# A fixed order for the first stage of a two-layer hybrid encoder, gates in tiles, the softmax ahead

## The chip, the cores and the metric

One core of one Trainium2 chip runs the whole network in one launch. The metric is the device time of that launch in microseconds (us), the median of several runs. TensorE (PE) multiplies matrices; VectorE (DVE), ScalarE (ACT) and GpSimd (POOL) do the elementwise work; SyncE (SP) issues most transfers.

## The reference, cut to what matters

The input is 512 tokens by 1024 features in float32. Layer 0 has sliding-window attention with sinks beside an HGRN2 recurrence, layer 1 has chunked attention; each layer ends with a gated feed-forward network with a short convolution. The change touches layer 0 up to the end of its attention.

```python
y = rms_norm(h, nw[0])                      # per token, over 1024 features, times a weight
proj = y @ w_in                             # split into qa, ka, va, qb, fb, ib, gb
# HGRN2, per head of 128 keys, in blocks of 32 tokens:
f = lb + (1 - lb) * sigmoid(f_logit); k = 1 - f
q_dec = q * exp(cumsum(log f)); k_dec = k * exp(-cumsum(log f))
s = where(causal, q_dec @ k_dec.T, 0); o = s @ ib + q_dec @ state    # state decays per block
# sliding-window attention, per head and 128 queries, after rotary embedding:
m = max(max(s), sink); p = exp(s - m); p = p / (sum(p) + exp(sink - m)); o = p @ va
```

## The kernel before, in words

Activations lie with features on the partitions (`xs`, eight chunks of 128 features by 512 tokens), weights come in units of 128 x 1024 float32. A product keeps close to float32 by a split: `prep` (L197) loads a unit, ScalarE rounds it to a high part (L206), VectorE takes the rest as the low part (L207), and `mm3` (L235) multiplies three times, high by high (L238), then the two cross terms (L239, L240). So 128 tokens against a panel of 512 columns take 24 matmuls of 512 columns over the 1024 features.

The order on each engine is set by a planner that walks the instructions by priority at compile time and keeps a model of when each is ready; the list of background steps (`later`, `fill`, `need`) sets which projection is written between which steps of a head.

`start` (L364) is the first stage. It runs 17 warm-up matmuls, loads four tiles of 128 tokens (L386) and the norm weight spread over all partitions (L303), and for each tile takes the sum of squares (L309), the root (L324 to L328), the product with norm weight and root (L343 for the first tile, on POOL at L345 and ScalarE at L348 for the others), eight transposes (L354) and the split (L357, L358). `value_panel` (L502) then makes the recurrence's values, tile by tile, and copies them to `ib` (L512).

`even` (L516) runs, for each of four heads, the projections `forget` and `query` in `hgrn_in` (L569), then `hgrn` (L609). In `forget` VectorE scans the decay `F` (L583), takes one reciprocal of 128 x 512 (L584), multiplies it with `kk` (L585), POOL makes a second product (L587), and VectorE fills a small table `tab` (L589 to L592). In `hgrn` the products of keys and values come from L643, VectorE turns them into running states `S` (L648, L650), and PE uses these at L656, between matmuls of the block's own scores (L654).

Then comes the rotary embedding (`rope`, L671: L679 on VectorE, L680 on POOL, L681 adds) and the attention. Each step `score` (L706) writes 128 queries' scores (L714, L715), adds the mask and takes the maximum on VectorE (L721), combines it with the sink (L722), exponentiates on ScalarE (L723), and divides (L724, L725); some steps later PE transposes the result (L734).

Of the kernel before, what the change touches and what calls it, by code (L numbers as in the profile page):

```python
# [27 lines left out]
P = 128  # L28
T = 512
# [11 lines left out]
HB = 32  # L41
HALF = (slice(0, 64), slice(64, 128))
TOK = [slice(t * P, (t + 1) * P) for t in range(NT)]
FH = [slice(0, 512), slice(512, 1024)]
# [101 lines left out]
class Net:  # L146
# [50 lines left out]
    def prep(self, i):  # L197
        if i in self.prepped or i >= len(UNITS):
            return
        nc, n = self.nc, UNIT_W[i]  # L200
        raw = self.wp.tile([P, UW], F32, tag="raw", bufs=3, name=f"wr{i}")
        hi = self.wp.tile([P, UW], F32R, tag="hi", name=f"wh{i}")
        lo = self.wp.tile([P, UW], F32R, tag="lo", name=f"wl{i}")
        o = int(UNIT_OFF[i]) * P
        nc.sync.dma_start(raw[:, :n], self.w[o:o + n * P].rearrange("(p n) -> p n", p=P))
# [76 lines left out]
    def rsqrt(self, nv, n=1):  # L282

        v = self.nc.vector
        y, t = self.small(n, "rs"), self.small(n, "rt")
        v.tensor_scalar(y.bitcast(I32), nv.bitcast(I32), -0.5, RSQRT_SEED, op0=ALU.mult, op1=ALU.add)
        for _ in range(3):
            if n == 1:

                v.tensor_scalar(t, y, y, nv, op0=ALU.mult, op1=ALU.mult)  # L290
                v.tensor_scalar(y, t, 1.5, y, op0=ALU.add, op1=ALU.mult)
            else:
                v.tensor_mul(t, y, nv)
                v.tensor_mul(t, t, y)
                v.scalar_tensor_tensor(y, t, 1.5, y, op0=ALU.add, op1=ALU.mult)
# [40 lines left out]
    def pre_norm(self, t, src, w, x, first=False):  # L336
# [4 lines left out]
        if first:  # L341
            r = self.root(s)
            nc.vector.scalar_tensor_tensor(hw, src, r, w, op0=ALU.mult, op1=ALU.mult)  # L343
        else:
            nc.gpsimd.tensor_mul(hw, src, w)  # L345
            r = self.root(s)
            for f in FH:
                nc.scalar.mul(hw[:, f], hw[:, f], r)  # L348

        def turn():  # L350
            for a in range(2):
                ps = self.bank("t", 2)
                for k in range(4):
                    nc.tensor.transpose(ps[:, TOK[k]], hw[:, (4 * a + k) * P:(4 * a + k + 1) * P], self.ident)  # L354
                at = lambda z: z[:, 4 * a:4 * a + 4, TOK[t]]
                p3 = ps.rearrange("p (k n) -> p k n", n=P)
                nc.scalar.copy(at(x[0]), p3)  # L357
                nc.vector.tensor_sub(at(x[1]), p3, at(x[0]).bitcast(F32))  # L358
        return turn
# [4 lines left out]
    def start(self):  # L364
        nc = self.nc
        self.ident = self.cp.tile([P, P], F32, name="ident")
        zeros = self.hp.tile([P, D], F32, tag="h3", name="zeros").bitcast(BF16)[:, :T]
        self.pt = self.cp.tile([P, PT_W], F32, name="pt")
        self.pt, self.eps = self.pt[:, :PC_N], self.pt[:, PC_N:PC_N + 1]
        nc.vector.memset(zeros, 0.0)  # L370
        nc.vector.memset(self.eps, EPS)
        make_identity(nc, self.ident)

        warm = self.small(1, "warm")
        nc.vector.memset(warm, 0.0)
        nc.scalar.activation(warm, warm, AF.Sqrt)
        ps = self.bank("s", 2)

        def warm_up(n):
            for _ in range(n):  # L380
                nc.tensor.matmul(ps, zeros[:, 0:P], zeros, start=True, stop=True)

        warm_up(17)
        x = self.new_x()
        src = [self.yp.tile([P, D], F32, tag="y", name=f"x{t}") for t in range(NT)]
        load = lambda t: nc.sync.dma_start(src[t], self.x[TOK[t], :])  # L386
        load(0)
        w = self.norm_row(0, 0)
        load(1)
        for i in range(NT):  # L390
            self.prep(i)
        load(2)
# [3 lines left out]
        for t in range(NT):  # L396
            self.turns[t] = self.pre_norm(t, src[t], w, x, t == 0)
            if t == 0:
                self.turn(0)
                warm_up(3)  # L400
        return self.chunks(x)
# [114 lines left out]
    def even(self, xs):  # L516
        nc, tc = self.nc, self.tc
        with tc.tile_pool(name="ev", bufs=2) as ep:
# [14 lines left out]
            lg = self.pt[:, PC_LB:PC_LB + 8]  # L533
            mx, e0, e1 = fix(4), fix(4), fix(4)
            nc.vector.tensor_max(mx, lg[:, 0:4], lg[:, 4:8])
            nc.vector.tensor_sub(e0, lg[:, 0:4], mx)
            nc.vector.tensor_sub(e1, lg[:, 4:8], mx)
            nc.scalar.activation(e0, e0, AF.Exp)
            nc.scalar.activation(e1, e1, AF.Exp)
            nc.vector.tensor_add(mx, e0, e1)  # L540
            nc.vector.reciprocal(mx, mx)
            c0, c1 = fix(4), fix(4)
            nc.vector.tensor_mul(c0, e0, mx)
            nc.vector.tensor_scalar(c1, c0, -0.5, 0.5, op0=ALU.mult, op1=ALU.add)
            nc.vector.tensor_scalar(c0, c0, 0.5, 0.5, op0=ALU.mult, op1=ALU.add)
            sink, nsink, hgn = self.pt[:, PC_SINK:PC_SINK + 8], fix(8), fix(4)
# [476 lines left out]
```

## Time and profile before

| | |
|---|---|
| median of 3 runs | 1220.49 us (1220.44 to 1220.56) |
| the profiled execution's own time | 1220.75 us |
| its span, first to last instruction | 1219.0 us |
| mean granted TensorE clock | 0.997 of 2.4 GHz |
| busy: PE, VectorE, ScalarE, POOL | 98%, 53%, 44%, 11% |

How to read it: busy time is the union of an engine's instructions in the span. A matmul's end is modelled, so PE can be called busy while the next matmul is already overdue; the distance from one matmul's start to the next one's is the surer measure. A row of the timeline gives start, duration, engine, line, operation, tiles written and read, a count, and in brackets the idle time before it and what ended that.

### The profile page before, as it was taken

Reading aid. Unit: us, or ns where it says so; the run is one execution under the profiler, and the core shown is the slowest. Engines: PE = TensorE matmul, PEld = TensorE weight load, DVE = VectorE, ACT = ScalarE, POOL = GpSimd, SP = SyncE. Lnnn points to the kernel's source line nnn. Section 1 sums busy time; section 2 is a strip of 40 time slices with the busy share of each in tenths; the row PEclk is TensorE's granted clock in tenths of the full one; section 3 lists DMA queues with packets and bytes.
Section 4 is the critical chain, followed back from the end, with each engine's and each line's share of the span. In section 5 each row is a group of like instructions: output and inputs, shape, how many; then the busy total and the mean of one; then the engine's idle time right before and its main releaser. Section 6 shows DMA issues by size and latency. Waiting matters only on the chain.

```text
span 1219.0 us, 15387 instructions
## 1 busy us (share of the span) xinstructions
PE 1198.4 (98%) x5804; PEld 982.6 (81%) x5804; DVE 649.9 (53%) x1317; ACT 536.9 (44%) x979; POOL 131.5 (11%) x127
## 2 busy tenths in 40 slices
PE   8999999999999999999999999999999999999997
PEld 5878777898888888888887777778888888888886
DVE  6687785755542244453457766756544522444434
ACT  6334564653332233333556656556533322333331
POOL 4233210320000000001420000003200000000011
PEclk9999999999999999999999999999999999999999
DMA  7413311234222332222243223212332223332211
GB/s 251 137 54 113 113 62 52 81 128 137 87 95 81 112 110 87 104 89 84 80 132 105 75 60 121 96 51 87 115 121 103 80 95 104 104 104 87 95 61 70
DMA packets 35595, 119.53 MB, mean 98 GB/s; under 512 B 4160, under 2 KB 4288, under 8 KB 35520
## 3 DMA queue, kind: packets, MB, share of 16 engines
q1 hardware_dynamic: 34944, 117.49, 29.3%
q8 instruction: 46, 0.75, 0.2%
q10 hardware_dynamic: 576, 1.05, 0.2%
q14 instruction: 29, 0.24, 0.1%
HBM read 115.12 MB, written 2.10 MB: 96 GB/s over the span
## 4 chain that ended last, share of the span: by engine, by line
PE 85%; DVE 6%; ACT 3%; issue 3%; POOL 2%; DMA 1%; SPq 0%; DVEq 0%; ACTq 0%; POOLq 0%
PE ps_mm L238 17%; PE ps_mm L239 17%; PE ps_mm L240 17%; PE ps_s L238 4%; PE ps_s L239 4%; PE ps_s L240 4%; PE ps_po L238 3%; PE ps_po L240 3%; PE ps_po L239 3%; PE ps_mm L956 2%; PE ps_po L902 2%; PE ps_t L891 1%; DVE wl L207 1%; POOL hw L345 1%; DVE hg L584 1%
## 5 line engine op out<-in xcount | busy, mean ns | idle before, releaser
L207 DVE TENSOR_TENSOR wl<-wr,wh 128x1024 fp32r<-128x1024 f32 (+1 forms) x191 | 235.9, 1237 | 319.3 <-ACT wh L206 314.0
L206 ACT CAST wh<-wr 128x1024 fp32r<-128x1024 f32 x198 | 204.4, 1035 | 371.2 <-PE ps_mm L239 116.0
L238 PE MATMUL ps_mm<-xh,wh 128*128 128x512 f32 x608 | 242.8, 399 | 0.0
L239 PE MATMUL ps_mm<-xl,wh 128*128 128x512 f32 x608 | 238.1, 392 | 0.0
L240 PE MATMUL ps_mm<-xh,wl 128*128 128x512 f32 x608 | 237.9, 391 | 0.0
L240 PEld LDWEIGHTS ps_mm<-xh,wl 128*128 128x128 f32 x608 | 114.2, 188 | 24.1 <-issue 0.4
L238 PEld LDWEIGHTS ps_mm<-xh,wh 128*128 128x128 f32 x608 | 114.5, 188 | 21.3 <-issue 0.9
L239 PEld LDWEIGHTS ps_mm<-xl,wh 128*128 128x128 f32 x608 | 114.5, 188 | 20.0
L238 PE MATMUL ps_mm<-wh,ah 128*128 128x512 f32 x264 | 102.8, 389 | 0.0
L240 PE MATMUL ps_mm<-wh,al 128*128 128x512 f32 x264 | 102.7, 389 | 0.0
L239 PE MATMUL ps_mm<-wl,ah 128*128 128x512 f32 x264 | 102.7, 389 | 0.0
L437 POOL TENSOR_TENSOR y<-y,nw 128x512 f32<-128x512 f32 x16 | 22.2, 1394 | 675.6 <-ACT junk L309 675.6
L238 PE MATMUL ps_s<-xh,wh 128*128 128x512 f32 x208 | 80.9, 389 | 0.0
L239 PE MATMUL ps_s<-xl,wh 128*128 128x512 f32 x208 | 80.9, 389 | 0.0
L240 PE MATMUL ps_s<-xh,wl 128*128 128x512 f32 x208 | 80.9, 389 | 0.0
L932 ACT ACTIVATE g<-g 128x512 f32<-128x512 f32 x44 | 27.8, 632 | 84.0 <-DVE g L931 84.0
L240 PEld LDWEIGHTS ps_mm<-wh,al 128*128 128x128 f32 x264 | 49.5, 188 | 10.3
L239 PEld LDWEIGHTS ps_mm<-wl,ah 128*128 128x128 f32 x264 | 49.5, 188 | 10.3
L238 PEld LDWEIGHTS ps_mm<-wh,ah 128*128 128x128 f32 x264 | 49.6, 188 | 10.2
L933 DVE TENSOR_TENSOR a<-ps_mm,g 128x512 f32<-128x512 f32 x32 | 22.1, 692 | 55.7 <-PE ps_mm L240 55.4
L879 ACT ACTIVATE pr<-pr,m 128x128 f32<-128x128 f32 (+1 forms) x64 | 36.0, 563 | 33.7 <-DVE m L878 33.2
L240 PEld LDWEIGHTS ps_s<-xh,wl 128*128 128x128 f32 x208 | 39.0, 188 | 8.2
(245 smaller groups left out, 2065.6 us busy)
## 6 DMA issues: line engine op xcount, KB each, us to landing
wr<-in_w SPq DMA_DIRECT2D x190, 512.0 KB, 3.5
nw<-in_nw SPq DMA_DIRECT2D x8, 512.0 KB, 4.2
bt<-in_relb SPq DMA_DIRECT2D x16, 256.0 KB, 3.2
x<-in_x SPq DMA_DIRECT2D x4, 512.0 KB, 5.5
h<-in_x SPq DMA_DIRECT2D x4, 512.0 KB, 3.5
wr<-in_w SPq DMA_DIRECT2D x8, 256.0 KB, 2.5
rope<-rope SPq DMA_DIRECT2D x20, 64.0 KB, 2.0
out<-h SPq DMA_DIRECT2D x4, 256.0 KB, 2.0
```

What stands on the lines that cost most here:

```text
L206: nc.scalar.copy(hi[:, :n], raw[:, :n])
L207: (nc.gpsimd if i in POOL_LO else nc.vector).tensor_sub(lo[:, :n], raw[:, :n], hi[:, :n].bitcast(F32))
L238: mm(ps, a[0], b[0], start=start, stop=False, skip_group_check=skip)
L239: mm(ps, a[0], b[1], start=False, stop=False, skip_group_check=skip)
L240: mm(ps, a[1], b[0], start=False, stop=stop, skip_group_check=skip)
L345: nc.gpsimd.tensor_mul(hw, src, w)
L437: nc.gpsimd.tensor_mul(z, z, wy[:, FH[f]])
L879: nc.scalar.activation(p_, p_, AF.Exp, bias=m, accum_out=den)
L902: nc.tensor.matmul(po[rows, j * P:], v[j][:, o:o + 64], pT[g][:, po_[j]:po_[j] + T - j * P], start=j == 0, stop=j == 3, skip_group_check=True)
L932: nc.scalar.activation(g, g, AF.Gelu)
L933: nc.vector.tensor_mul(a, pv, g)
L956: nc.tensor.matmul(ps[:, hf], u[wi][:, k, :], xs[k][xi][:, hf], start=i == k == 0, stop=i == 2 and k == KD - 1, skip_group_check=True)
```

## The change

The first stage is written as one method, `opening`, in a block where PE, VectorE and ScalarE keep the written order. The first token tile is multiplied raw: transposed as loaded, weighted by the norm weight per partition while it leaves PSUM (`weighted`), and multiplied in plain float32 with the unsplit weight units (`plain`, eight matmuls of 512 columns); its root is applied to the result, and to the tile itself later, by a product with a row of roots that PE spreads with a matmul of ones. The second tile is scaled by its root, transposed, and weighted per partition in the same way. The third and fourth are scaled by VectorE alone. The warm-up falls from 17 and 3 matmuls to 7, 1 and 2. The transfers are issued in the order x0, norm row (8 x 128, from ScalarE's queue), units 0 and 1, x1, units 2 and 3, x2, spread norm weight, x3, parameters, and units 0 to 2 land in buffers that are free, so none of these waits. What follows the opening (units 4 to 6, the small gate constants) is issued behind its last instructions.

In `forget` the table comes before the reciprocal, and reciprocal and product run in four tiles of 128 columns. In `hgrn` the copy of the transposed keys and the states `S` get a priority of 300 ahead, in `score` the whole softmax. The sine product of the rotary embedding moves from POOL to VectorE.

```diff
-        def turn():
-            for a in range(2):
-                ps = self.bank("t", 2)
...
+        load(0)
+        nc.scalar.dma_start(rows, self.nw[0, 0].rearrange("(k n) -> k n", n=P))
+        self.fetch(0, raw[0])
+        self.fetch(1, raw[1])
+        load(1)
+        self.fetch(2, raw[2])
+        self.fetch(3, raw[3])
+        load(2)
+        w = self.norm_row(0, 0)
+        load(3)
...
+        def scaled(t):
+            hw[t] = self.wide("hw")
+            for f in FH:
+                nc.vector.scalar_tensor_tensor(hw[t][:, f], src[t][:, f], r[t], w[:, f], op0=ALU.mult, op1=ALU.mult)
...
+        def weighted(out, ps):
+
+            for a in range(2):
+                nc.vector.tensor_mul(p3(out[:, FH[a]]), p3(ps[a]),
+                                     wcol[:, 4 * a:4 * a + 4].unsqueeze(2).to_broadcast([P, 4, P]))
...
+        with self.tc.manual_schedule(engines={E.PE, E.DVE, E.Activation}):
...
+            warm_up(7)
...
+            pt = [self.turn_half(src[0], a) for a in range(2)]
+            warm_up(2)
+            weighted(x0, pt)
+            nc.scalar.copy(hi[0], raw[0])
+            part_lo(0)
+            nc.scalar.copy(hi[1], raw[1])
+            part_lo(1)
+            r[1] = self.root(self.square_sum(src[1]))
+            p0 = self.bank("mm", 3)
+
+            def plain(k):
+                nc.tensor.matmul(p0, x0[:, TOK8[k]], raw[k // 2][:, FH[k % 2]], start=k == 0, stop=k == KD - 1)
+
+            for k in range(5):
+                plain(k)
+            hw[1] = self.wide("hw")
+            pt = []
+            for a in range(2):
+                nc.vector.tensor_scalar_mul(hw[1][:, FH[a]], src[1][:, FH[a]], r[1])
+                pt.append(self.turn_half(hw[1], a))
+            for k in range(5, KD):
+                plain(k)
+            nc.scalar.copy(hi[2], raw[2])
+            x1 = self.wide("x1")
+            weighted(x1, pt)
...
+            r[2] = self.root(self.square_sum(src[2]))
+            scaled(2)
...
+            p1 = self.tok(ps1, xs, us, 1, True, True)
+            for _ in range(7):
+                next(p1)
+            self.to_features(2, hw[2], x)
+            self.run_all(p1)
+            r[0] = self.root(self.square_sum(src[0]))
+            r[3] = self.root(self.square_sum(src[3]))
+            scaled(3)
...
+            p2 = self.tok(ps2, xs, us, 2, True, True)
+            for _ in range(6):
+                next(p2)
+            self.to_features(3, hw[3], x)
+
+            pr = self.bank("po", 1)
+            nc.tensor.matmul(pr[:, 0:P], ones, diag, start=True, stop=True)
+            self.run_all(p2)
+            x3 = p3(x0)
+            nc.vector.tensor_mul(x3, x3, pr[:, 0:P].unsqueeze(1).to_broadcast([P, KD, P]))
+            for a in range(2):
+                nc.scalar.copy(at(x[0], 0, a), x3[:, 4 * a:4 * a + 4])
+                end = [nc.vector.tensor_sub(at(x[1], 0, a), x3[:, 4 * a:4 * a + 4], at(x[0], 0, a).bitcast(F32))]
+            end.append(nc.scalar.copy(ib[2], ps2))
+
+        self.opened = [i.ins for i in end]
+        with self.behind():
+            for i in range(4, 7):
+                self.prep(i)
+        ps3 = self.bank("mm", 3)
+        self.run_all(self.tok(ps3, xs, us, 3, True, True))
...
-                    nc.vector.reciprocal(kd, F)
-                    nc.vector.tensor_mul(kd, kd, kk)
...
+                    for t in range(NT):
+                        nc.vector.reciprocal(kd[:, TOK[t]], F[:, TOK[t]])
+                        nc.vector.tensor_mul(kd[:, TOK[t]], kd[:, TOK[t]], kk[:, TOK[t]])
+
+                    nc.gpsimd.tensor_mul(blk(f2), blk(kd), blk(F)[:, :, HB - 1:].to_broadcast([P, T // HB, HB]))
...
+                with self.tc.high_priority(AHEAD):
+                    for t in range(NT - 1):
+                        S.append(ep.tile([P, P], F32, tag="S", bufs=3, name="S"))
...
-                    nc.gpsimd.tensor_mul(sw, sw, cst[:, CC_SIN:CC_SIN + T])
+                    nc.vector.tensor_mul(sw, sw, cst[:, CC_SIN:CC_SIN + T])
...
+                with self.tc.high_priority(AHEAD):
+                    nc.vector.tensor_tensor_reduce(p_, ps[:, :n], am[:, 256 - n:], 1.0, NEG, ALU.add, ALU.max, m)
+                    nc.vector.tensor_scalar(nm, m, -1.0, nsink[:, hh:hh + 1], op0=ALU.mult, op1=ALU.min)
```

## Rows read from the trace of the kernel before

**Rows 1.** The page: busy time of the engines, and the chain that ended last.
```profile
PE 1198.4 (98%) x5804; PEld 982.6 (81%) x5804; DVE 649.9 (53%) x1317; ACT 536.9 (44%) x979; POOL 131.5 (11%) x127
...
PE 85%; DVE 6%; ACT 3%; issue 3%; POOL 2%; DMA 1%; SPq 0%; DVEq 0%; ACTq 0%; POOLq 0%
```
**Rows 2.** PE's waits over the span: for whom, us in total, times, longest us.
```profile
PE ps_po L656 <- DVE S L650: 2.1, 6, 0.5
PE ps_t L734 <- DVE pr L725: 1.9, 2, 1.2
...
PE ps_po L656 <- DVE S L648: 1.0, 1, 1.0
...
PE ps_s L714 <- DVE qa L788: 0.5, 1, 0.5
PE ps_s L714 <- DVE m L721: 0.4, 1, 0.4
```
**Rows 3.** Stretches: length, busy of PE, PEld, DVE, ACT, POOL, PE's clock, DMA.
```profile
4.30:11.10 6.80, 4.16 (x23) 2.12 (x21) 3.59 (x10) 4.55 (x9) 2.99 (x4) 1.00 1.00 374
11.10:14.50 3.40, 3.25 (x7) 2.00 (x7) 3.40 (x5) 3.40 (x6) 2.48 (x3) 0.50 0.83 259
...
136.00:200.00 64.00, 61.09 (x340) 46.91 (x340) 55.32 (x202) 41.48 (x115) 12.28 (x31) 1.00 0.24 76
```
**Rows 4.** Timeline of PE from 0 to 13.5 us: transposes and first product.
```profile
8.20 1.06 PE L354 MATMUL ps_t<-ident,hw 128*128 128x128 f32 x8 [1.00 <-DVE hw L343]
10.90 0.62 PE L238 MATMUL ps_mm<-wh,xh 128*128 128x512 f32 x1 [1.64 <-ACT xh L357]
```
**Rows 5.** Timeline from 0 to 25 us: two sums of squares, the second root's end.
```profile
4.49 1.06 ACT L309 ACTIVATE junk<-x 128x1024 bf16<-128x1024 f32 x1 [2.26 <-DMA x<-in_x]
...
7.96 1.06 ACT L309 ACTIVATE junk<-x 128x1024 bf16<-128x1024 f32 x1 [1.99 <-DMA x<-in_x]
...
9.97 0.21 DVE L328 TENSOR_SCALAR rs<-rt,rs 128x1 f32<-128x1 f32 x1
```
**Rows 6.** Timeline of PE from 38 to 39.5 us: values end, first gate begins.
```profile
38.28 0.39 PE L238 MATMUL ps_mm<-wh,xh 128*128 128x512 f32 x1
...
38.96 0.39 PE L238 MATMUL ps_mm<-xh,wh 128*128 128x512 f32 x1
```
**Rows 7.** VectorE's groups by shape, 0 to 40 us: count, busy us, mean ns, idle.
```profile
L358 DVE TENSOR_TENSOR xl<-ps_t,xh 128x512 fp32r<-128x512 f32 x8 | 5.2, 684 | 1.7 <-ACT xh L357 1.7
```
**Rows 8.** ScalarE's groups by shape, 0 to 40 us.
```profile
L206 ACT CAST wh<-wr 128x1024 fp32r<-128x1024 f32 x8 | 8.4, 1050 | 1.4 <-PE ps_mm L240 1.4
```
**Rows 9.** VectorE's groups by shape, 40 to 215 us.
```profile
L207 DVE TENSOR_TENSOR wl<-wr,wh 128x1024 fp32r<-128x1024 f32 x23 | 28.0, 1218 | 17.8 <-ACT wh L206 17.4
L584 DVE RECIPROCAL hg<-hg 128x512 f32<-128x512 f32 x4 | 13.4, 3339 | 0.0
```
**Rows 10.** Timeline of PE from 70 to 79 us: plain float32 products, two records each.
```profile
74.76 1.05 PE L618 MATMUL ps_t<-qd,hg 128*128 128x128 f32 x8
75.65 0.33 PE L622 MATMUL ps_s<-qd,hg 128*128 128x64 f32 x2
```
**Rows 11.** Timeline from 60 to 69 us: the second gate beside the first head's states.
```profile
64.58 0.60 PE L654 MATMUL ps_po<-ib,sz 128*128 128x128 f32 x4
...
66.18 0.46 PE L656 MATMUL ps_po<-S,hg 128*128 128x128 f32 x2 [1.00 <-DVE S L648]
...
66.56 0.16 DVE L590 TENSOR_TENSOR tab<-tab 128x8 f32<-128x8 f32 x1
...
66.78 1.14 POOL L587 TENSOR_TENSOR hg<-hg 128x512 f32<-128x512 f32 x1 [5.94 <-DVE tab L590]
66.90 1.05 DVE L591 TENSOR_TENSOR tab<-tab 128x8 f32<-128x8 f32 x1
```
**Rows 12.** Timeline from 146 to 150 us: a division of the softmax beside POOL.
```profile
147.25 1.37 DVE L725 TENSOR_SCALAR pr<-pr,den 128x128 f32<-128x128 f32 x1
147.27 1.27 POOL L680 TENSOR_TENSOR rope<-rope,cst 128x512 f32<-128x512 f32 x1
```

More of the change, by code (lines that the diff above doesn't have):

```diff
@@ L8 @@
 from collections import deque
-from contextlib import ExitStack
+from contextlib import ExitStack, contextmanager
 import numpy as np
@@ L41 @@
 HB = 32
+AHEAD = 300
 HALF = (slice(0, 64), slice(64, 128))
 TOK = [slice(t * P, (t + 1) * P) for t in range(NT)]
+TOK8 = [slice(k * P, (k + 1) * P) for k in range(KD)]
 FH = [slice(0, 512), slice(512, 1024)]
@@ L334, in new_x, with pre_norm @@
         return xh, xl
-    def pre_norm(self, t, src, w, x, first=False):
+    def pre_norm(self, t, src, w, x):
         nc = self.nc
@@ L359, in pre_norm, with turn_half, halve @@
-        return turn
+        nc.gpsimd.tensor_mul(hw, src, w)
+        r = self.root(s)
+        for f in FH:
+            nc.scalar.mul(hw[:, f], hw[:, f], r)
+        return lambda: self.to_features(t, hw, x)
+    def turn_half(self, hw, a):
+        ps = self.bank("t", 2)
+        for k in range(4):
+            self.nc.tensor.transpose(ps[:, TOK[k]], hw[:, (4 * a + k) * P:(4 * a + k + 1) * P], self.ident)
+        return ps
+    def halve(self, t, a, src, x):
+        at = lambda z: z[:, 4 * a:4 * a + 4, TOK[t]]
+        p3 = src.rearrange("p (k n) -> p k n", n=P)
+        self.nc.scalar.copy(at(x[0]), p3)
+        self.nc.vector.tensor_sub(at(x[1]), p3, at(x[0]).bitcast(F32))
@@ L361, in chunks, with to_features, opening @@
+    def to_features(self, t, hw, x):
+        for a in range(2):
+            self.halve(t, a, self.turn_half(hw, a), x)
     def chunks(self, x):
         return [(x[0][:, k, :], x[1][:, k, :]) for k in range(KD)]
-    def start(self):
+    def opening(self):
         nc = self.nc
+        scratch = self.hp.tile([P, D], F32, tag="h3", name="scratch")
+        zeros, ones, diag = scratch[:, A].bitcast(BF16), scratch[:, 256:384], scratch[:, 384:512]
+        rows, wcol = scratch[0:KD, 512:640], scratch[:, 640:640 + KD]
@@ L370, in start @@
+        load = lambda t: nc.sync.dma_start(src[t], self.x[TOK[t], :])
         nc.vector.memset(zeros, 0.0)
@@ L372, in start @@
         make_identity(nc, self.ident)
[L374 to L386, printed above, removed]
-        load(0)
+        nc.gpsimd.memset(ones, 1.0)
+        load(0)
+        nc.scalar.dma_start(rows, self.nw[0, 0].rearrange("(k n) -> k n", n=P))
[5 more added lines that the diff above has]
+        load(2)
         w = self.norm_row(0, 0)
[L389 to L392, printed above, removed]
         load(3)
@@ L395, in start, with part_lo @@
         self.turns = [None] * NT
[L396 to L401, printed above, removed]
+        hi, lo = ([self.wp.tile([P, UW], F32R, tag=z, name=f"w{z}{i}") for i in range(4)] for z in ("hi", "lo"))
+        hw, r = [None] * NT, [None] * NT
+        def part_lo(i):
+            nc.vector.tensor_sub(lo[i], raw[i], hi[i].bitcast(F32))
+            self.prepped[i] = (hi[i], lo[i])
@@ L403, in turn, with behind @@
+        self.opened = [i.ins for i in end]
[4 more added lines that the diff above has]
+        self.run_all(self.tok(ps3, xs, us, 3, True, True))
+        nc.scalar.copy(ib[3], ps3)
+        return xs, ib
+    @contextmanager
+    def behind(self):
+        with ExitStack() as s:
+            for i in self.opened:
+                s.enter_context(self.tc.issue_after(i))
+            yield
     def turn(self, t):
@@ L978, in run @@
     def run(self):
-        xs = self.start()
-        xs = self.even(xs)
+        xs = self.even(*self.opening())
         xs = self.ffn(0, xs, (1, 0))
```

139 lines of the change are left out of this document (77 added, 62 removed).

## The prediction

> **What bounds the kernel now.** Read the page first: PE is busy 98% of the span and holds 85% of the chain that ended last [rows 1]. Only two things can then move the time: less work on PE, or less time in which PE stands while its operands are late. So the views in their order are PE's waits (where it stands), the stretches (which engine is full there, and PE's clock), and the timeline beside each wait. The waits are few, and all of those that the change can touch lie before 200 us: the recurrence's states S, the softmax's result, the rotated queries [rows 2], and the first stage, which is best read by starts. There real work begins with the transposes at 8.20 [rows 4] and ends where the first gate projection starts, at 38.96 [rows 6]: 30.8 us. Its work is 96 matmuls of 0.227 (three take 38.28 to 38.96 [rows 6]) and 32 transposes of 0.11, estimated from 1.06 us for eight less the last one's modelled tail [rows 4]: 21.8 + 3.5 = 25.3 us. So 5.5 us are lost, partly in idling (1.00 and 1.64 us [rows 4]), partly in 3.4 us at a granted clock of 0.50, the 1.2 GHz level, after a stretch in which PE worked 4.16 of 6.80 us [rows 3].
>
> **The opening, step by step.** Prices: a plain float32 matmul of 128 columns takes 0.22 us (four take 74.76 to 75.65 [rows 10]), so 512 columns 0.89 us, against 24 x 0.227 = 5.45 us for one tile split: the raw tile costs PE 8 x 0.89 = 7.1 us, 1.7 more, and is paid back only by starting early. VectorE takes 0.68 us for 512 elements out of PSUM [rows 7]; a split unit takes 1.05 us on ScalarE [rows 8] and 1.22 on VectorE [rows 9]; a root takes 2.2 us from the start of its square to its end (7.96 to 10.18 [rows 5]). Transfers move 374 GB/s [rows 3], so 512 KB take 1.4 us; x0 is there at 4.49 [rows 5], and in the new order units 0 and 1 come at 5.9 and 7.3, x1 at 8.7, units 2 and 3 at 10.1 and 11.5. The new order on SP holds no wait before x3, so nothing stands behind a busy buffer; the norm row is small and on another queue.
> PE, then: eight transposes of x0 from 4.5; the first half is weighted by 5.8; `plain` begins at 5.9, with unit 0. Four take until 9.5, the fifth waits for unit 2 (10.1) and ends at 11.0. The second tile's root starts with x1 at 8.7 and is done at 10.9; VectorE scales its halves by 11.5 and 12.0 (0.55 each, my value between 0.34 and 0.68, half of and all of the PSUM price, nearer the latter since one operation is the nearest row); eight transposes end at 12.5, so PE stands 0.6. Three more `plain`: 15.2. Meanwhile VectorE weights and splits the second tile (four times 0.68, until about 14.9). Seven steps of three matmuls (4.8): 20.0. The third tile's root follows the split of units 2 and 3 on VectorE (17.3), plus 0.9 and 2 x 0.68: 19.6, in time. Transposes and the last step: 21.6. Six steps: 25.7. The fourth tile is VectorE's next debt: its two squares, two roots and scaling follow ScalarE's copies of the third (21.5): 2 x 1.5 us on ScalarE, 0.9 and 1.4 on VectorE: 26.8, so PE stands about 0.7; transposes 27.4, the matmul of ones 0.2, two steps 1.4: 28.9. The fourth tile's 24 matmuls, 5.45 us: 34.4. By then the raw tile has its root (1.3 us, then two halves of 0.6 and 0.7: 31.9), and unit 4, held behind that, is split at 31.9 + 1.05 + 1.22 = 34.2, just in time. The first gate starts at 34.4 in place of 38.96: **4.6 us gained**. Bounds: with no stand at all after 5.9, 7.1 + 72 x 0.227 + 24 x 0.11 + 0.2 = 26.3, so 32.2 and 6.8 gained; with the stands above doubled (2.0 more) and a drop of the clock (below) 0.9 gained. What covers unit 4 is the fourth tile; if VectorE is late there, every us late is a us lost.
>
> **The gates.** PE waits for S seven times. The reciprocal of 3.34 us [rows 9] stands in VectorE's queue when S is wanted, and all behind it waits. The waits count 2.1 + 1.0 = 3.1 us [rows 2]; by starts each is 0.16 longer, since the four records of L654 from 64.58 end a step of 0.11 later, at 65.02, and L656 starts at 66.18: 1.16 where the row says 1.00 [rows 11]. So 3.1 + 7 x 0.17 = 4.3 us. In tiles, a piece takes 3.34 / 4 = 0.84 and at most 0.16 more (the small operation's price [rows 11]), and S, with its priority, goes between pieces: it is ready about 1 us earlier than PE needs it. What is late next is POOL's product, which now follows four pairs of 1.0 + 0.25 in place of 3.34 + 0.67: 1 us later, more where S cuts in. Only the first head has little time for that, since its own matmuls follow at once; I take 0.7 (between 0 and 1.6). **3.6 us gained**, between 2.7 and 4.3 by these ends, and 1.5 if S in the seven cases still meets a piece and waits its 0.16.
> The table's operations are now ahead of the reciprocal. One of them, L591, takes 1.05 us where its like, L590, takes 0.16; it ends together with POOL's product, 66.78 + 1.14 [rows 11]. Read by its row, it would cost its 1.05 anywhere and POOL's start would be 0.9 us later still in the first head, a gain of 2.7. The Trainium skill (SBUF — State Buffer, "SBUF: two separate sides") says that VectorE and GpSimd share one pair of ports as an exclusive lock, held for a whole instruction, also by a VectorE operation with two SBUF inputs against a GpSimd one that reads SBUF. By that rule L591 has waited for the lock, and costs 0.16 ahead of the product; the common end in the trace bears this out, and I keep 3.6.
>
> **The softmax.** PE waits 1.9 us for the division L725, 0.5 for the rotated queries, 0.4 for the maximum [rows 2], four waits, by starts 0.17 more each: 3.5 us. The longest stands beside POOL's sine product: L725 takes 1.37 us for 128 columns while L680 runs its 1.27 from 147.27 [rows 12]. With that product on VectorE (0.68 in place of 1.27, nearest row L358 [rows 7]) the partner is gone, and the queries' chain is some 0.6 shorter. Added: five products of 0.68 on VectorE, 3.4 us, beside PE's projections; they cost only where the softmax is due at once, and the priority lets it pass all but one already running. I take 0.6 (0 to 2.8, half of the waits and the remainder). **2.9 us gained**, between 0.7 and 3.5.
>
> **Sum.** 4.6 + 3.6 + 2.9 = 11.1; the profiled execution took 1220.75 (span 1219.0 and 1.75 around it), so 1209.65; the median is 0.26 below that execution: **1209.4 us**. Everything after 200 us keeps its work and is only moved.
>
> **The rivals.**
> Clock: PE stands or works thinly in the opening and the clock falls again. For it: it fell to 0.50 for 3.4 us [rows 3] after idling of 1.00 and 1.64 us [rows 4], and only 10 warm-ups are left of 20. Against: the longest stand I find is 0.7. A spell at half clock costs 1.7; with units arriving late (1 us) the opening gains 1.9: 1212.1. The Trainium skill (TensorE: Matmul & The Clock Gate, "Part 1: The HAM clock gate (the "warmup" mystery)") has the throttled clock as the default, which activity releases; the fall after the thin stretch in the trace agrees.
> Moved waits: the written order and the priorities shift what is late to the weights' split and to POOL. The gates then gain 1.5 and the softmax 0.7: 1220.5 - 6.8 = 1213.7. For it: both stages rest on the planner's model of time; against: each wait removed has a cause in the rows that goes with it.
> VectorE as the bound, on the other side: from 136 to 200 us it is busy 55.32 of 64 us [rows 3]. With three sine products (2.0) in 64 - 3.5 us it would be at 57.3 of 60.5, 95%. If the softmax, always ahead, drives it to 100%, each weight unit's split slides behind it, and PE meets its weights late by both halves, 1.05 + 1.22 = 2.27 us, at about ten units: 23 us against 8.2 gained before: 1235. Against: VectorE's weights are written two units ahead.
> No effect: the planner already reached this order, 1220.5. Against: the raw tile alone changes the first stage.
>
> **How the numbers follow.** A measurement of this kernel tells some 0.2% (2.4 us) from no change. Forecast 0.60, its own range 1206.5 to 1212; more than that, towards the bounds 6.8 + 4.3 + 3.5 = 14.6 (1205.9), 0.05; clock 0.14; moved waits 0.12; no effect 0.04; VectorE 0.05. The range from 1205.5 to 1215.5 takes in the first four cases with their spread. Faster 0.91, same 0.04, slower 0.05.
>
> **What would show it.** The first gate's first matmul near 34.4; `plain` records from about 5.9; a granted clock of 1.00 from 4.3 on; no wait of PE for S above 0.3 us; no L725 above 0.5 us; the first head's POOL product about 1 us later against its scan. Wrong if the first gate starts after 37, if PE's waits for S stay above 2 us together, or if PE waits for `wl` between 130 and 200 us.

## The result, and the profile after

The changed kernel takes 1211.49 us (median of 4 executions, 1211.12 to 1212.55), the kernel before 1220.49 us beside it: a ratio of 0.9927 (95% interval 0.9915 to 0.9938), 9.0 us less. The forecast was 1209.4. The profiled execution is the longest of the four, 1212.55 us with a span of 1210.8. In two kernels below one execution of five ran in a slower state (`no_state_priority` 1489.05 us, `mask_first_held` 1305.7 us), and the medians and ratios given leave it out.

The page of the changed kernel: busy time of the engines, and the chain that ended last. They answer to [rows 1].

```profile
PE 1195.8 (99%) x5789; PEld 979.3 (81%) x5789; DVE 656.1 (54%) x1356; ACT 534.5 (44%) x975; POOL 111.8 (9%) x120
...
PE 89%; DVE 3%; issue 3%; ACT 2%; POOL 2%; DMA 1%; SPq 0%; DVEq 0%; ACTq 0%; POOLq 0%
```

PE's waits in the changed kernel, over the span (whom it waited for, us in total, times, the longest), against [rows 2]:

```profile
PE ps_po L783 <- DVE S L775: 2.1, 3, 0.9
...
PE ps_s L749 <- DVE hg L684: 0.9, 1, 0.9
PE ps_mm L456 <- DVE nv L330: 0.6, 1, 0.6
...
PE ps_t L356 <- DVE hw L463: 0.4, 1, 0.4
```

The waits for the softmax's division, for the rotated queries and for the maximum are gone. Those for S (L775 makes S[0]) are fewer but not shorter: three of up to 0.9 us, where seven of up to 1.0 were forecast to vanish. And there is one that no row of before has, L749 for `q2` (L684).

Three stretches of the changed kernel (length; busy of PE, PEld, DVE, ACT, POOL; PE's clock; DMA), the first two those of [rows 3], the third the attention, 8 us earlier:

```profile
4.30:11.10 6.80, 6.18 (x22) 3.05 (x22) 4.16 (x8) 3.79 (x6) 0.00 (x0) 1.00 0.99 393
11.10:14.50 3.40, 2.98 (x14) 1.55 (x13) 2.83 (x7) 1.52 (x3) 0.00 (x0) 1.00 1.00 364
128.00:192.50 64.50, 64.48 (x355) 49.06 (x354) 56.49 (x205) 43.13 (x118) 7.28 (x28) 1.00 0.26 84
```

PE works 6.18 us of the first stretch in place of 4.16, and the granted clock keeps its upper level in the second, where before it fell to half. In the attention PE is full while VectorE has 8 us to spare.

Where the 9.0 us come from is read best from the starts of marked matmuls of PE, each less the same one's start before (us; from the timelines). A head's own scores are the products of `kd` with `qd`, its first products that need the gate; its far scores, against earlier blocks of the same 128 tokens, follow.

| kernel | first gate | own scores, heads 1 / 2 / 3 | last weighing of values | last matmul |
|---|---|---|---|---|
| the changed kernel | -4.07 | -4.12 / -4.61 / -5.06 | -7.98 | -8.13 |
| opening alone | -5.13 | -4.10 / -4.13 / -4.16 | -3.83 | -3.90 |
| gates alone | 0.07 | -0.96 / -1.46 / -1.93 | -1.40 | -1.38 |
| softmax alone | -0.10 | -0.10 / -0.14 / -0.14 | -3.09 | -3.23 |

After the last weighing all of them only shift what follows.

### The profile page after: what moved, and what is told of

It is laid out like the page before. It is cut to its first block, busy times and chain, and to the rows that moved or that the text cites. A ratio compares the mean times of both kernels' runs of the same rounds, so it can differ in the third digit from the quotient of the medians.

```text
span 1210.8 us, 15381 instructions
## 1 busy us (share of the span) xinstructions
PE 1195.8 (99%) x5789; PEld 979.3 (81%) x5789; DVE 656.1 (54%) x1356; ACT 534.5 (44%) x975; POOL 111.8 (9%) x120
## 4 chain that ended last, share of the span: by engine, by line
PE 89%; DVE 3%; issue 3%; ACT 2%; POOL 2%; DMA 1%; SPq 0%; DVEq 0%; ACTq 0%; POOLq 0%
PE ps_mm L248 18%; PE ps_mm L250 18%; PE ps_mm L249 18%; PE ps_s L248 4%; PE ps_s L250 4%; PE ps_s L249 4%; PE ps_po L248 3%; PE ps_po L250 3%; PE ps_po L249 3%; PE ps_po L1030 2%; POOL hw L346 2%; PE ps_t L1019 1%; PE ps_mm L1084 1%; PE ps_s L1001 1%; PE ps_s L1002 1%
## 5 line engine op out<-in xcount | busy, mean ns | idle before, releaser
L217 DVE TENSOR_TENSOR wl<-wr,wh 128x1024 fp32r<-128x1024 f32 (+1 forms) x187 | 232.5, 1246 | 313.3 <-ACT wh L216 308.6
L216 ACT CAST wh<-wr 128x1024 fp32r<-128x1024 f32 x194 | 200.0, 1034 | 370.1 <-PE ps_mm L249 109.8
```

## The experiments

All of them compute the reference's outputs in full.

**One part of the change at a time.** Three kernels: the changed one with gates and softmax as before (`open_only`), and the one before with the gates alone and with the softmax alone.

> The opening of the changed kernel with the gates and the softmax of the kernel before. Sum of parts (each part gives what its stage shows in the two traces): the first gate starts near 34.9 us as in the changed kernel, against 38.96 before, and the time is 1220.5 - 4.1 = 1216.4 us (1215.4 to 1216.6, since runs of the changed kernel differ by more than those of before). Rival, a fixed opening changes what the planner does later as well: the time is 1214 us or less, or 1218 or more, with the first gate at the same place.

> The kernel before with the gates alone changed: table first, reciprocal and product in four tiles, states and transposed keys ahead. My forecast: 3.6 us gained, 1216.9 us. Reading of the trace after (PE's waits for S by starts 3.4 us where it had 4.3, and a new wait of 1.0 us in the first head): 0 to 1 us gained, 1219.5 to 1220.5 us, with a wait of PE for S of 0.7 to 1.1 us in each of three heads.

> The kernel before with the softmax alone changed: priority, the sink's minimum as a scalar operation, sine product on VectorE. My forecast: 2.9 us gained, 1217.6 us. Reading of the trace after, where none of the four waits is left: 3.5 us gained, 1217.0 us, no wait of PE for the division, the queries or the maximum. Rival, VectorE is full and the weights' split slides: 1219 us or more with PE waiting for the low parts of weights.

What `open_only` takes back from the changed kernel; `gates_only` and `soft_only` have the same lines the other way round, the first down to the states, the second from the sine product on:

```diff
+                    nc.vector.reciprocal(kd, F)
+                    nc.vector.tensor_mul(kd, kd, kk)
...
-                    for t in range(NT):
-                        nc.vector.reciprocal(kd[:, TOK[t]], F[:, TOK[t]])
-                        nc.vector.tensor_mul(kd[:, TOK[t]], kd[:, TOK[t]], kk[:, TOK[t]])
...
-                with self.tc.high_priority(AHEAD):
-                    for t in range(NT - 1):
...
-                    nc.vector.tensor_mul(sw, sw, cst[:, CC_SIN:CC_SIN + T])
+                    nc.gpsimd.tensor_mul(sw, sw, cst[:, CC_SIN:CC_SIN + T])
...
-                with self.tc.high_priority(AHEAD):
-                    nc.vector.tensor_tensor_reduce(p_, ps[:, :n], am[:, 256 - n:], 1.0, NEG, ALU.add, ALU.max, m)
```

Measured: opening 1217.08 us (0.9972, 0.9962 to 0.9983), gates 1219.35 (0.9989, 0.9981 to 0.9998), softmax 1217.56 (0.9976, 0.9966 to 0.9985), beside 1220.51 for the kernel before: 3.43, 1.16 and 2.95 us gained. The softmax came out as forecast; the opening reached its forecast at the first gate and then lost a microsecond; the gates gave a third of theirs. The opening's time lies outside the range expected for it, and between that and its rival's. The three add up to 7.5, not 9.0. PE's waits of `open_only`, from 40 to 135 us, show where the opening loses its microsecond:

```profile
PE ps_s L747 <- DVE tab L715: 0.4, 1, 0.4
PE ps_s L745 <- POOL hg L710: 0.2, 1, 0.2
```

They fall on head 0's far scores, 0.94 us by starts (the distance from the start of the matmul before, less its usual step). The scan of head 0's gate starts 10.23 us after the first gate there (44.06 less 33.83), 9.20 in the kernel before (48.16 less 38.96), so the lead shrinks from 5.13 to 4.10 us between the first gate and head 1. That is not what the sum lacks, though: in the changed kernel the scan starts 10.19 us after the first gate (45.08 less 34.89), and PE loses 1.02 us on the same far scores, to `q2`, while `gates_only` loses nothing there. What the sum lacks lies behind head 3's own scores. From there to the last weighing the changed kernel gains 2.92 us and the softmax alone 2.95, but the opening alone loses 0.33 and the gates alone 0.53, together 0.83 us less than the changed kernel. In `gates_only` head 3 waits for S as well, 0.49 and 0.37 us by starts, which the changed kernel does not. PE's waits there, 40 to 135 us, the last of the four in head 3:

```profile
PE ps_po L662 <- DVE S L654: 2.4, 4, 0.9
```

The rest of the difference is open; executions of one opening differ by up to 1.3 us at the first gate (below).

**Which half of the softmax's part.** The sine product alone on VectorE, and the priority alone, each on the kernel before. The third edit of this part, the minimum with the sink as another VectorE operation, is in neither.

> The kernel before with one line changed: the sine product of the rotary embedding on VectorE in place of POOL. Lock theory: three of the four waits of the first attention (0.60, 1.32 and 0.87 us by starts) stand beside POOL's sine product and go with it, and the queries are earlier, so most of what the softmax part gave alone (2.95 us) is here: 2.3 to 3.0 us gained, 1217.5 to 1218.2 us. Priority theory: the product matters little, 0 to 0.8 us gained, 1219.7 to 1220.5 us.

> The kernel before with the softmax's priority alone, sine product left on POOL. Lock theory: the waits beside POOL's product stay, 0 to 0.7 us gained, 1219.8 to 1220.5 us, and VectorE's division of 128 columns still takes over 1 us once. Priority theory: 2 us or more gained, 1218.5 us or less.

```diff
-                    nc.gpsimd.tensor_mul(sw, sw, cst[:, CC_SIN:CC_SIN + T])
+                    nc.vector.tensor_mul(sw, sw, cst[:, CC_SIN:CC_SIN + T])
```

```diff
-                nc.vector.tensor_tensor_reduce(p_, ps[:, :n], am[:, 256 - n:], 1.0, NEG, ALU.add, ALU.max, m)
+                with self.tc.high_priority(AHEAD):
+                    nc.vector.tensor_tensor_reduce(p_, ps[:, :n], am[:, 256 - n:], 1.0, NEG, ALU.add, ALU.max, m)
...
+                    nc.vector.tensor_scalar_mul(p_, p_, den)
```

Measured: 1217.93 us (0.9978, 0.9969 to 0.9987) for the product, 1219.54 (0.9992, 0.9983 to 1.0) for the priority. So moving the sine products off POOL gives 2.65 of the 2.95 us; the priority by itself gives 1.0, and its executions spread from 1218.66 to 1221.37, so its share is not settled. In `priority_only` PE still waits for the division (L728 here), although it has the priority, because it is not late in the queue but slow. PE's wait, then VectorE's divisions of 140 to 160 us, then POOL, 140 to 152 us:

```profile
PE ps_t L737 <- DVE pr L728: 1.1, 1, 1.1
```

```profile
139.93 0.29 DVE L728 TENSOR_SCALAR pr<-pr,den 128x128 f32<-128x128 f32 x1
...
147.35 1.37 DVE L728 TENSOR_SCALAR pr<-pr,den 128x128 f32<-128x128 f32 x1
```

```profile
147.37 1.27 POOL L682 TENSOR_TENSOR rope<-rope,cst 128x512 f32<-128x512 f32 x1
```

In `sine_only` that wait is gone. VectorE's groups there, 130 to 200 us, show the division of 128 columns at a mean of 281 ns (the sine products at 680). In the kernel before, the slow one stood beside POOL's sine product in the same way [rows 12].

```profile
L680 DVE TENSOR_TENSOR rope<-rope,cst 128x512 f32<-128x512 f32 x4 | 2.7, 680 | 0.0
...
L725 DVE TENSOR_SCALAR pr<-pr,den 128x128 f32<-128x128 f32 x8 | 2.2, 281 | 0.0
```

**Is it the pieces?** The changed kernel with one reciprocal of 512 columns again, behind the table.

> The changed kernel with the reciprocal and its product in one piece of 512 columns again; table first, priorities and all else kept. Theory of the order: the pieces are what lets the states in, so the wait for the states grows back by 0.3 to 0.5 us in each of three heads, time 1212.4 to 1213.0 us. Rival, the table ahead gives it: within 0.4 us of 1211.5.

```diff
-                    for t in range(NT):
-                        nc.vector.reciprocal(kd[:, TOK[t]], F[:, TOK[t]])
-                        nc.vector.tensor_mul(kd[:, TOK[t]], kd[:, TOK[t]], kk[:, TOK[t]])
+                    nc.vector.reciprocal(kd, F)
+                    nc.vector.tensor_mul(kd, kd, kk)
```

Measured: 1213.08 us (0.994, 0.9928 to 0.9952), about 1.6 slower than the changed kernel by medians; no execution of either reaches into the other's range, but the two intervals overlap. PE's waits, 40 to 135 us:

```profile
PE ps_po L782 <- DVE tab L709: 1.6, 3, 0.9
PE ps_po L782 <- DVE S L776: 0.9, 4, 0.4
```

L782 reads S, not the table. The first row names `tab` because that operation ended last; what PE waits for is S[0], whose copy starts at 61.74 in head 0, right behind a reciprocal that runs from 58.48 to 61.82. By starts the waits for S are 2.04, 0.71 and 0.94 us in heads 0 to 2, where the changed kernel has 1.37, 1.02 and 1.01. By these waits the pieces help in head 0 alone.

**Is it that S stands behind the third piece?** In VectorE's queue S[0] stands behind the third piece and S[2] behind the fourth. First, pieces three and four of heads 1 to 3 held behind the last state; then S without its priority, which puts S[0] behind all four pieces; then the masked copy of the own scores at the states' priority, which lets S pass the third piece; and this together with the hold.

> The changed kernel, but the last two pieces of the reciprocal and POOL's products of heads 1 to 3 are issued behind the three states S of the head before. Theory of the order (S is late because the written queue holds it behind the third piece, although its products are there 2.4 us earlier): PE's waits for S by starts fall from 3.4 to under 0.6 us, time 1211.5 - 2.9 = 1208.6 us. Rival, the pieces hold VectorE and POOL anyway, so the wait moves to the next head's products or to the weights: time within 0.5 us of 1211.5.

> The changed kernel without the priority of the three states S: the priority of the copy of ke, the four reciprocal pieces and all else stay. VectorE's order then has S[0] behind all four pieces and their products, S[1] behind the query's product and S[2] behind q2. Theory (what the pieces pay is only what the place of the states pays): each of heads 0 to 2 loses one more piece and its product ahead of S[0], 0.94 + 0.15 us, so the waits for S by starts go from 3.4 to about 6.7 us, more than the 4.3 to 5.0 of before, and the time from 1211.5 to about 1214.8 us. Rival (the pieces pay because the tables and the queries come earlier, whatever the states do): 1211.5 to 1212 us, waits for S as in the changed kernel.

> The changed kernel with the masked copy of the own scores into sz (VectorE) put at the same priority as the states. It then stands ahead of the next head's gate in VectorE's queue, and by the written order S[0] of heads 0 to 2 stands ahead of the third piece and S[2] ahead of the fourth. Theory (the states are late because they stand behind reciprocal pieces): the waits for S fall from 3.4 us by starts to about 1 us, 1209.1 us, and the copy of ke on ScalarE comes earlier with the masked copy. Rival (each gap closed in a head is paid in the next, because VectorE is the engine that sets the pace of heads 1 to 3): 1211 to 1212 us, with new waits for the query's product or the far scores.

> The kernel that holds the third and fourth piece of heads 1 to 3 behind the last state (1212.25 us), with the masked copy of the own scores put ahead as well. There head 0's wait for S fell from 1.37 to 0.29 us and head 1 gave it back as 1.37 us (0.47 in head 2) of the products' wait for ScalarE's copy of ke, which stood behind two copies that waited for the masked copy. Theory (that queue is the cause): these 1.84 us go and no wait for S above 0.3 stays, 1212.25 - 1.84 - 1.5 = 1208.9 us, at least 1210.4. Rival (VectorE sets the pace): the held pieces come too late for the next head's own scores, which then wait for kd, and the time stays at 1212 us or above.

The hold, and the states without their priority:

```diff
+                if h < 3:
+                    with self.tc.issue_after(last.ins):
+                        self.rest()
```

```diff
-                with self.tc.high_priority(AHEAD):
-                    for t in range(NT - 1):
...
+                for t in range(NT - 1):
```

Here `last` is the last state and `rest` takes the two pieces and POOL's products. The masked copy:

```diff
-                nc.vector.copy_predicated(sz.rearrange("p (t n) -> p t n", n=P),
...
+                with self.tc.high_priority(AHEAD):
+                    nc.vector.copy_predicated(sz.rearrange("p (t n) -> p t n", n=P),
```

Measured: 1212.25, 1211.71, 1212.83 and 1214.07 us (0.9936, 0.9927, 0.9934, 0.9944). None is faster than the changed kernel, and the theories that set the time by S's place in the queue fall. In the first, head 0's wait for S fell from 1.37 to 0.29 us by starts (in heads 1 and 2 the wait for S[0] stays, 0.76 and 0.75), and head 1 gave it back at the products of keys and values, which wait for ScalarE's copy:

```profile
PE ps_s L780 <- ACT hg L776: 1.5, 2, 1.2
```

Without its priority S[0] is waited for 1.62, 0.71 and 1.01 us by starts in heads 0 to 2 (1.10, 0.74 and 0.74 in the changed kernel), the later states hardly at all: 3.5 us together in place of 3.4, not the 6.7 of the theory, and nothing is lost at head 3. The reason is in front of the gate, not behind it: in that order the gate's tanh passes the weight split, and the scan of head 2's gate starts 0.46 us earlier. VectorE in `no_state_priority`, 71 to 76 us, and in the changed kernel, 72 to 82 us:

```profile
71.56 0.55 DVE L701 TENSOR_SCALAR hg<-hg,fix 128x512 f32<-128x512 f32 x1 [1.70 <-ACT hg L700]
...
74.91 1.21 DVE L705 TENSOR_TENSOR_SCAN hg<-hg,dd 128x512 f32<-128x512 f32 x1
```

```profile
72.68 1.23 DVE L217 TENSOR_TENSOR wl<-wr,wh 128x1024 fp32r<-128x1024 f32 x1 [2.14 <-ACT wh L216]
73.83 0.54 DVE L701 TENSOR_SCALAR hg<-hg,fix 128x512 f32<-128x512 f32 x1
...
75.37 1.23 DVE L705 TENSOR_TENSOR_SCAN hg<-hg,dd 128x512 f32<-128x512 f32 x1
...
79.13 0.94 DVE L714 RECIPROCAL hg<-hg 128x128 f32<-128x128 f32 x1
79.99 0.22 DVE L775 COPY S<-ps_s 128x128 f32<-128x128 f32 x1
```

In the changed kernel VectorE is idle for 2.14 us in front of head 2's gate, because the low part of a weight unit (L217) heads its queue and waits for ScalarE's rounding (L216), which itself stands behind the output copies of head 0. ScalarE there, 70 to 73 us, where the gate's own tanh (L700) comes last:

```profile
70.57 1.14 ACT L792 ACTIVATE ob<-ps_po,rs 128x128 f32<-128x128 f32 x4 [4.09 <-DVE rs L300]
71.59 1.06 ACT L216 CAST wh<-wr 128x1024 fp32r<-128x1024 f32 x1
72.53 0.62 ACT L700 ACTIVATE hg<-ps_mm 128x512 f32<-128x512 f32 x1
```

In `mask_first` PE reaches head 1 1.29 us earlier than in the changed kernel (69.35 against 70.64; 0.30 of it from the opening), but the masked copy now stands ahead of the gate and the scan starts at 75.54, 0.17 later than 75.37; PE then waits 1.22 us for S[0].

```profile
79.54 0.46 PE L784 MATMUL ps_po<-S,hg 128*128 128x128 f32 x2 [1.05 <-DVE S L776]
```

A new theory follows: heads 0 to 2 are paced by a chain that goes round once a head: S, its use, ScalarE's squares, the root on VectorE, ScalarE's output copies, the weight split, the next head's gate and scan, its pieces, and the next S. Moving S alone moves no time, if something else in the chain moves the other way.

**The chain, cut in another place.** One ordering edge: in heads 1 to 3 the split of the weight unit that the query fetches ahead is queued behind the head's own gate. S stays behind all but the last products of the pieces.

> The changed kernel with one ordering edge more: the split of the weight unit that the query of heads 1 to 3 fetches ahead (ScalarE's rounding copy, VectorE's residue) is queued behind that head's gate, on ScalarE behind the tanh and on VectorE behind the last reciprocal product, where the changed kernel has it ahead of the gate (in head 0 a residue of 2.07 us, in heads 1 and 2 a rounding copy of 1.06 and a residue of 1.23 us between the normalised output and the gate). Theory (the pace of heads 0 to 2 is set by a chain, states, squares, root, output copies on ScalarE, weight split, gate of the next head, states, and the states' own place in VectorE's order moves nothing by itself): the scan of head 1's gate starts about 3 us earlier, of heads 2 and 3 about 1.7 us earlier; the wait for q2 (1.02 us) and most of the waits for S (3.4 us by starts) go, 0.4 us stays: 1211.5 - 4.0 = 1207.5 us. Rival (VectorE has no slack there, and work put off in a head comes back in the next): waits for wl or for the query's product appear in place of these, and the time stays at 1211 to 1212.5 us.

```diff
-    def feat(self, xs, take, bank=None):
+    def feat(self, xs, take, bank=None, hold=None):
...
-        u = self.unit()
+        with ExitStack() as s:
+            for i in hold or []:
+                s.enter_context(self.tc.issue_after(i))
+            u = self.unit()
...
-                    nc.scalar.activation(f2, ps, AF.Tanh, scale=0.5)
+                    hold.append(nc.scalar.activation(f2, ps, AF.Tanh, scale=0.5).ins)
...
+                    hold.append(end.ins)
...
-                yield from self.feat(xs, query)
+                yield from self.feat(xs, query, hold=hold if h else None)
```

Here `end` is the last product of the four pieces.

Measured: 1209.62 us (0.9916, 0.9902 to 0.993; five executions from 1209.24 to 1211.49), the fastest kernel here, 1.9 us below the changed one's median. The two intervals against the kernel before overlap (the ratios alone are 1.3 us apart), and the two were not run side by side, so the size is not settled; the place where it gains is shown by the trace. PE's waits, 40 to 135 us, then VectorE, 68 to 80 us:

```profile
PE ps_po L786 <- DVE sz L763: 1.3, 1, 1.3
PE ps_po L788 <- DVE S L780: 0.3, 1, 0.3
```

```profile
68.63 0.55 DVE L704 TENSOR_SCALAR hg<-hg,fix 128x512 f32<-128x512 f32 x1 [1.69 <-ACT hg L703]
...
70.14 1.91 DVE L708 TENSOR_TENSOR_SCAN hg<-hg,dd 128x512 f32<-128x512 f32 x1
...
74.60 1.74 DVE L717 RECIPROCAL hg<-hg 128x128 f32<-128x128 f32 x2
76.27 0.22 DVE L780 COPY S<-ps_s 128x128 f32<-128x128 f32 x1
```

S[0] stands behind all four pieces, one more than in the changed kernel, and PE waits for it once, for 0.48 us by starts; the wait for `q2` is gone too. The scan of head 2's gate starts 2.97 us after head 1's own scores (70.14 less 67.17) where it was 4.73 (75.37 less 70.64): 1.76 earlier, as forecast (in head 1's gate it is 4.2 earlier where 3 was forecast, in head 3's 1.3 where it was 1.7). VectorE still idles 1.69 us in front of the gate, now for the gate's own tanh. From the first gate to head 3's own scores the kernel takes 67.93 us, the changed one 70.50, the one before 71.49. Of these 2.57 us 2.49 are gained between the own scores of heads 0 and 1, where the changed kernel waits 1.02 us for `q2` and 1.37 for S. The forecast of 1207.5 was missed by 2.1 us. Of it 1.45 is a wait that was not foreseen: in head 2 the copy of the far scores (L763) was put behind the states and the weight split.

```profile
94.45 1.22 DVE L217 TENSOR_TENSOR wl<-wr,wh 128x1024 fp32r<-128x1024 f32 x1
95.58 0.41 DVE L763 COPY sz<-ps_s 64x256 f32<-64x256 f32 x1
```

**The second tile earlier.** In the opening PE stands 0.6 and 0.4 us around the second tile. The changed kernel with x1 loaded ahead of unit 1 and the root ahead of that unit's split:

> The changed kernel with the second token tile loaded before weight unit 1, and its square and root ahead of unit 1's split on ScalarE and VectorE. Theory of the transfer: in the profiled execution unit 1 came at 8.1 us and x1 at 9.4, in two others at 7.0 and 8.2 to 8.5, and the first gate started at 34.9 against 33.8 to 34.0, so the second root hangs on x1 and on the queue ahead of it. Then the root ends near 9.3 in every execution, PE's gap before the second tile's transposes goes, the first gate starts at 33.6 to 33.9, the time is 1210.9 us (1210.6 to 1211.2) with less spread. Rival, the third weight unit or the clock holds the opening: the first gate stays between 33.8 and 34.9, the time at 1211.5.

```diff
+        load(1)
         self.fetch(1, raw[1])
-        load(1)
...
+            r[1] = self.root(self.square_sum(src[1]))
             nc.scalar.copy(hi[1], raw[1])
-            part_lo(1)
-            r[1] = self.root(self.square_sum(src[1]))
...
+            part_lo(1)
```

Measured: 1211.68 us (0.9927, 0.9914 to 0.9941), no difference. Both stands are gone, but the eight transposes of the first tile took 1.91 us in this profiled execution and 1.10 in the changed kernel's; PE's timelines of 4 to 13 us, first this kernel's, then the changed kernel's:

```profile
4.90 1.91 PE L356 MATMUL ps_t<-ident,x 128*128 128x128 f32 x8
...
7.32 4.46 PE L455 MATMUL ps_mm<-wr,x 128*128 128x512 f32 x10
11.61 1.04 PE L356 MATMUL ps_t<-ident,hw 128*128 128x128 f32 x8
```

```profile
4.90 1.10 PE L356 MATMUL ps_t<-ident,x 128*128 128x128 f32 x8
...
6.34 3.79 PE L456 MATMUL ps_mm<-wr,x 128*128 128x512 f32 x8
10.75 1.10 PE L456 MATMUL ps_mm<-wr,x 128*128 128x512 f32 x2 [0.62 <-DVE nv L330]
12.26 1.06 PE L356 MATMUL ps_t<-ident,hw 128*128 128x128 f32 x8 [0.42 <-DVE hw L463]
```

The first gate starts at 34.21 against 34.89, and what the order gains in a usual execution can't be told from the spread.

## Why the prediction was right, and which term was mis-sized

The time and the sign were right: 1209.4 forecast, 1211.49 measured, inside the range. Two terms of the sum held and one did not. The range is 10 us wide and would have held the time with nothing at all from the gates (1220.5 - 7.5 = 1213.0), so the hit says nothing for that term.

**The opening.** Forecast 34.4 for the first gate. In the profiled executions of the eight kernels with this very opening it starts between 33.68 and 34.94 (34.89 in the changed one), 4.0 to 5.3 us earlier than before where 4.6 was forecast. The steps fit as well: `plain` from 6.34 (5.9 forecast), the fifth one late for its unit (10.75; 10.1 forecast; the row names `nv`, which this product does not read, and the unit landed at 10.62), the second tile's transposes at 12.26 (11.5 to 12.5 forecast). No stand of more than 0.8 us is in it. The clock did not fall again, so the rival that cost 2.7 us did not come: with the new opening, PE busy for 6.18 of 6.80 us in the changed kernel, no profile shows a fall before the end of the kernel, also not the two whose clock rose as early as 3.96 and 4.45 us; with the old one all four that rose before 5 us fell between 10.8 and 11.6, and the fifth, which rose at 6.89, did not fall. The Trainium skill's rule that the prediction weighed there (TensorE: Matmul & The Clock Gate, Part 1: throttled by default, released by activity) agrees with both. What goes with the early and the late first gates is the transfer of unit 1, forecast for 7.3 us. ScalarE's rounding of that unit, which waits for it, starts at 7.82 to 8.12 us in the three kernels whose first gate is at 34.59 to 34.94, and at 6.85 to 7.13 in the five at 33.68 to 34.13. ScalarE in the changed kernel, then in `open_only`:

```profile
8.12 1.04 ACT L450 CAST whi<-wr 128x1024 fp32r<-128x1024 f32 x1 [1.36 <-DMA wr<-in_w]
```

```profile
6.92 1.05 ACT L450 CAST whi<-wr 128x1024 fp32r<-128x1024 f32 x1 [0.22 <-DMA wr<-in_w]
```

Why the transfer lands at two times in kernels with the same opening is open.

**The softmax.** Forecast 2.9, measured 2.95 alone. The reason was right too, and `sine_only` shows it without the priority. The division's shape has a mean of 281 ns in `sine_only`; in the changed kernel, 128 to 200 us, it is

```profile
L853 DVE TENSOR_SCALAR pr<-pr,den 128x128 f32<-128x128 f32 x8 | 2.3, 284 | 0.0
```

and before (VectorE's groups, 136 to 206 us)

```profile
L725 DVE TENSOR_SCALAR pr<-pr,den 128x128 f32<-128x128 f32 x8 | 3.4, 421 | 0.0
```

The prediction used the rule of an exclusive lock between VectorE and GpSimd (the Trainium skill, SBUF — State Buffer, "SBUF: two separate sides") for operations with two SBUF inputs. The division reads one tensor and a scalar per partition, and was held up beside POOL as well; the same passage of the Trainium skill names operations in a 2-port perf mode too, and whether the division ran in that mode no run here shows. The table's small operations, by the same rule 0.16 us ahead of POOL's product, take 0.10 to 0.16 there.

**The gates.** Forecast 3.6, measured 1.16 alone; in the changed kernel the lead grows by 0.99 us from the first gate to head 3's own scores. The step that failed is: "S, with its priority, goes between pieces: it is ready about 1 us earlier than PE needs it." S does go between pieces, but it is ready 0.74 to 1.10 us after PE needs it, by starts, and again 0.27 to 0.28 later in each of heads 0 to 2: 3.4 us stay, of 4.8 in the kernel before by the same measure (4.3 in the prediction's reckoning). The prediction's own sign of being wrong came here, "if PE's waits for S stay above 2 us together": 2.1 us by the profile's row, 3.4 by starts. The step took the reciprocal for the cause because S stood behind it. The runs show that the place of S by itself gains nothing (1211.71 without its priority) and that the start of the gate counts: with the weight split behind it the scan of head 2's gate starts 1.76 us earlier against head 1's own scores, and the waits for S fall from 3.4 to 0.48 us, though S stands one piece later. The waits' releaser, S, does not name that split. The prediction's lowest figure for the term, 1.5, is near what was measured, but by luck: seven times its price of 0.16, taken from 3.6, leaves 2.5. What it priced as late next, POOL's product one microsecond later in head 0, did not come: it starts 5.82 us after the scan (50.90 less 45.08), 5.97 before (54.13 less 48.16). What was late instead is beside it. In head 0 of the changed kernel, POOL, then VectorE:

```profile
50.90 1.09 POOL L717 TENSOR_TENSOR hg<-hg 128x512 f32<-128x512 f32 x1 [6.12 <-DVE hg L715]
```

```profile
51.27 1.79 DVE L217 TENSOR_TENSOR wl<-wr,wh 128x1024 fp32r<-128x1024 f32 x1
52.98 0.83 DVE L684 TENSOR_TENSOR hg<-qd,tab 128x256 f32<-128x256 f32 x1
```

The weight split, 1.79 us beside POOL's product in place of 1.23, stands ahead of `q2`, and PE waits 1.02 us by starts for that. The table ahead of the reciprocal and the priority of the transposed keys are taken out by themselves in no run, so what they give within the term is not known.

**The rivals.** VectorE as the bound did not come: 56.49 us of 64.50 in the attention, and no wait for `wl` there. Moved waits came in one stage of two: the gates gave even less than that rival's 1.5 when alone, the softmax gave all. That the parts alone sum to 7.5 us and together give 9.0 was in no term of the forecast, and it made up for part of what the gates lack: 0.83 us of it are lost behind head 3's own scores when opening and gates stand alone, the rest is open.

## What to carry to other kernels

A wait's releaser is the last step of a chain; before pricing a cure at that step, follow the chain back through each queue to where an engine idles, here 2.14 us in front of the gate, behind a weight split that nothing needed yet. Test it by changing the order there: one ordering edge gave 1.9 us by medians (the intervals overlap), where four kernels that moved the named operation gave nothing or lost. And where VectorE is slow beside GpSimd, move the GpSimd operation first; priority did not cure a slow instruction.

## What was not expected of the hardware

The prediction reckoned with a hold-up by GpSimd only for VectorE operations that read two tensors. The division, which reads one, is held up too: 128 columns take 0.28 us alone and 1.37 beside POOL's sine product, although by the records it starts 0.02 us before that [rows 12]. And the start of PE's upper clock differs between executions: by the records of the granted clock it is first given at 3.96 to 7.16 us in the profiled kernels here, 4.30 in the one before, 5.01 in the changed one and 7.16 in the kernel with x1 earlier, whose eight transposes at the same 4.90 us took 1.10 and 1.91 us. It does not settle when the opening ends: with the very same opening, a clock from 3.96, 5.01 and 7.05 us goes with a first gate at 33.90, 34.89 and 34.13.
